# Long convolutions: four real products in PSUM, transform additions on VectorE, and full tables for the first inverse class

## The chip, the cores and the metric

The kernel runs on one core of one Trainium2 chip, as one launch. The metric is the device time in microseconds (us). Three runs of the kernel before gave 2213.26, 2218.42 and 2222.65 us; the median, 2218.42 us, is the time before.

## The reference

Two transformer layers run one after the other on a sequence of 1024 positions with 1024 channels, all in 32-bit floats. The first mixes dilated window attention with a Hyena branch, the second a state-space branch with latent attention. The change lies in the Hyena branch of the first layer alone: two rounds of a bidirectional long convolution over 512 channels, each followed by a gate, whose filters come from a small network.

```python
def bidirectional_long_conv(z, h_fwd, h_bwd):
    circ = jnp.concatenate([h_fwd, jnp.zeros((1, C), jnp.float32), h_bwd[:0:-1]], axis=0)
    hf = jnp.fft.rfft(circ, axis=0)
    zf = jnp.fft.rfft(z.astype(jnp.float32), n=2 * L, axis=1)
    y = jnp.fft.irfft(zf * hf[None], n=2 * L, axis=1)[:, :L]
...
    z = v
    for o, gate_o in enumerate((x1, x2)):
        z = gate_o * (bidirectional_long_conv(z, filters[:, o, 0], filters[:, o, 1]) + filt_bias[o] * z)
```

## The kernel before

**The transform.** Each convolution is done in the frequency domain, for 256 of the 512 channels at a time (`HC`), so there are four convolutions (two orders, two halves) and four transforms of filters. The 2048 frequencies are split by their residue modulo 16. Additions of 128x256 tiles (class `Fly`, lines 483 to 510, used by `fwd16`, `fwd8` and `inv8`) first make nine classes of inputs, of which classes 0 and 8 share one tile. A matrix product on TensorE with a table of cosines and sines then does the rest of each class: 128 positions in, 128 frequencies out, real and imaginary part side by side in a tile of 128 x 2 x 256. `inv8` puts the classes together again after the inverse products.

**Precision.** A matrix product of 32-bit floats is done with operands split into a high part (rounded to `fp32r`) and a low part (the rest): `split` casts on ScalarE (L176) and subtracts on VectorE or GpSimd (L181). `mm3` (L184 to L191) then issues three products, high by high, high by low, low by high, for each term.

**A transform of classes 1 to 7** (`transformed`, L654) multiplies a complex input by a complex table with three real products instead of four. `parts` (L616) first adds real and imaginary part on GpSimd (`sum`, L623), splits the sum on ScalarE and GpSimd, and splits the two parts themselves on ScalarE and VectorE. TensorE then forms one product of the sum (tile `ha`) and two others (tile `hx`), nine instructions of 256 columns in all. ScalarE copies `ha` out of PSUM (`sa`, L674), and VectorE adds it to both halves of `hx` (L675), which also brings the result to SBUF.

**The filters** (`filters`, L733): four rounds, each with 16 short products that give the filter's values, `fwd16`, and eight transforms, whose result `sp` is stored in DRAM.

**A convolution** (`long_conv`, L805) goes through the eight classes in the order 0, 4, 7, 1, 6, 2, 5, 3. `forward` splits the class, reads the filter's spectrum `hs` and transforms. `inverse` multiplies by the spectrum (L821 on VectorE; L822 on GpSimd, or on VectorE for class 0), combines on GpSimd (`zz`, L826 and L827), splits, and transforms back into a tile `wb`. When classes j and 8 - j are both back, their sum `sm` is formed on VectorE (L859) and their difference `df` on GpSimd (L860). Before the last two classes are transformed back, `fwd8` of the next convolution is written.

**The additions** of `Fly.tt` (L494) are given to VectorE and GpSimd in turn; the multiply-adds (L506) are all on VectorE.

**The first inverse class** holds classes 0 and 8 in one tile, 64 rows each. Twelve products (L843) work on half the rows each, in pairs for the two halves, and ScalarE copies the two results out (L845).

**What sets the order.** Each engine works through its own queue in a fixed order. The order is not written by hand: a scheduler places the instructions by the dependencies and its own estimates, and fills TensorE's gaps with projection products (`pj`, 512 columns) of later parts of the program, whose weights are read (`raw`), split (`wh`, `wl`) and whose results are evacuated by ScalarE (L983) and VectorE (`tr`, L984). Tiles have a fixed number of buffers, `HX` = 5 of them in PSUM for the transforms.

Of the kernel before, what the change touches and what calls it, by code (L numbers as in the profile page):

```python
# [9 lines left out]
F32 = mybir.dt.float32  # L10
# [6 lines left out]
P = 128  # L17
# [14 lines left out]
HC = 256  # L32
# [7 lines left out]
def constants():  # L40
# [18 lines left out]
    iv = np.zeros((8, 128, 3, 128))  # L59
# [24 lines left out]
    iv[0, 64:, 1] = -s8[:, :64].T / 1024  # L84
    rel = np.abs(np.arange(256)[None, :] - 64 - np.arange(128)[:, None])
# [396 lines left out]
class Fly:  # L482


    def __init__(self, k, bufs):
        self.nc, self.pool, self.n, self.bufs = k.nc, k.ypool, 0, bufs
# [4 lines left out]
    def tt(self, a, b, op, out=None):  # L491
        out = self.new() if out is None else out
        self.n += 1
        (self.nc.gpsimd if self.n % 2 == 0 else self.nc.vector).tensor_tensor(out, a, b, op=op)  # L494
        return out
# [77 lines left out]
def inv8(fl, w0, w8, w4, sm, df):  # L573

    A = {j: sm[j][:, 0] for j in (1, 2, 3)}
    Bp = {j: sm[j][:, 1] for j in (1, 2, 3)}
    Ap = {j: df[j][:, 0] for j in (1, 2, 3)}
    B = {j: df[j][:, 1] for j in (1, 2, 3)}
    c, c1, c3 = CS[2], CS[1], CS[3]
    s1, s3 = c3, c1  # L580
    x = [None] * 8
    a0, b0 = fl.add(w0, w8), fl.sub(w0, w8)
    p, n = fl.add(a0, w4[:, 0]), fl.sub(a0, w4[:, 0])
    g, h = fl.add(p, A[2]), fl.sub(p, A[2])
# [12 lines left out]
    x[3], x[5] = fl.add(u, v), fl.sub(u, v)  # L597
    return x
# [17 lines left out]
def parts(k, src, both=False):  # L616

    nc = k.nc
    n = 3 if both else 2
    hi, lo = (k.spl.tile([P, 3 if k.any else 2, HC], F32R, name="y" + x, tag="y" + x, bufs=k.bufs["y"]) for x in "hl")  # L620
    if both:
        t = k.spl.tile([P, HC], F32, name="sum", tag="sum", bufs=k.bufs["sum"])
        (nc.gpsimd if SUMP else nc.vector).tensor_add(t, src[:, 0], src[:, 1])  # L623
    split(nc, hi[:, :2], lo[:, :2], src)
    if both:
        split(nc, hi[:, 2], lo[:, 2], t, lo_eng="pool" if SUML else "dve")
    return [[t[:, c] for c in range(n)] for t in (hi, lo)]
# [21 lines left out]
FB = dict(y=2, sum=2, sa=1, t=2)  # L649
CB = dict(y=3, sum=2, sa=2, t=3)  # L650
LEADF = 1
DFP = 1
MULP = 1
# [5 lines left out]
def transformed(k, t, y, back, out):  # L659

    (th, tl), (yh, yl) = t, y
    nc = k.nc
    term = lambda b, c: (th[:, b, :], tl[:, b, :], yh[c], yl[c])
    ps = k.hps.tile([P, 2, HC], F32, name="hx", tag="hx", bufs=HX)
    if len(yh) < 3:
        mm3(nc, ps[:, 0], [term(0, 0), term(1, 1)])
        mm3(nc, ps[:, 1], [term(0, 1), term(2, 0)])
        return ps
    pa = k.hps.tile([P, 2, HC], F32, name="ha", tag="hx", bufs=HX)[:, 0]
    mm3(nc, pa, [term(0, 2)])  # L670
    mm3(nc, ps[:, 0], [term(1, 1)])
    mm3(nc, ps[:, 1], [term(2, 0)])
    sa = k.spl.tile([P, HC], F32, name="sa", tag="sa", bufs=k.bufs["sa"])
    nc.scalar.copy(sa, pa)  # L674
    nc.vector.tensor_add(out, ps, sa.unsqueeze(1).to_broadcast([P, 2, HC]))  # L675
    return out


def spectrum(k, y, j, out):

    if j:
        return transformed(k, table(k, "k_fw", j), y, 0, out)
    yh, yl = y
    ps = k.hps.tile([P, 2, HC], F32, name="hx", tag="hx", bufs=HX)
    ts = [table(k, "k_fw", c) for c in (0, 8)]
    for b in range(2):
        mm3(k.nc, ps[:, b], [(th[:, b, :], tl[:, b, :], yh[c], yl[c]) for c, (th, tl) in enumerate(ts)])
    return ps
# [41 lines left out]
def filters(k):  # L730
# [4 lines left out]
    with ExitStack() as es:  # L735
# [5 lines left out]
        k.bufs, k.any = FB, bool(KF)  # L741
# [27 lines left out]
        for n, (hf, o) in enumerate(rounds):  # L769
# [4 lines left out]
            ahead = [parts(k, y[j], j in KF) for j in ORDER[:LEADS]]  # L774
            for i, j in enumerate(ORDER):
                if i + LEADS < 8:
                    ahead.append(parts(k, y[ORDER[i + LEADS]], ORDER[i + LEADS] in KF))
# [28 lines left out]
def long_conv(k, y, o, hf, z):  # L806
# [5 lines left out]
    def forward(j):  # L812
        yp = parts(k, y[j], j in KZ)
        hs = k.hpl.tile([P, 2, HC], F32, name="hs", tag="hs")
        nc.sync.dma_start(hs, k.spec[o, hf, j])
        t2 = k.prd.tile([P, 2, HC], F32, name="t2", tag="t2", bufs=T2)
        return hs, t2, spectrum(k, yp, j, t2)

    def inverse(j, hs, t2, ps):
        zz = k.prd.tile([P, 2, HC], F32, name="zz", tag="zz", bufs=ZZ)  # L820
        nc.vector.tensor_mul(zz, ps, hs[:, 0:1].to_broadcast([P, 2, HC]))  # L821
        (nc.gpsimd if MULP and ps is t2 else nc.vector).tensor_mul(t2, ps, hs[:, 1:2].to_broadcast([P, 2, HC]))  # L822
# [27 lines left out]
    for i, j in enumerate(order):  # L850
# [5 lines left out]
        if 0 < j < 4:  # L856
# [3 lines left out]
            (nc.gpsimd if DFP and j in KI else nc.vector).tensor_sub(df[j], w[j], w[8 - j])  # L860
# [5 lines left out]
def hyena(k):  # L866
# [6 lines left out]
    with ExitStack() as es:  # L873
# [48 lines left out]
        k.ybufs, k.bufs, k.any = YB, CB, bool(KZ or KI)  # L922
# [1298 lines left out]
```

## Time and profile before

| What | us |
|---|---|
| median of 3 runs | 2218.42 |
| the profiled execution's own time | 2230.01 |
| its span, first to last instruction | 2228.2 |
| TensorE (PE) busy in the span | 2046.7 (92%) |
| VectorE (DVE) busy | 1489.1 (67%) |
| ScalarE (ACT) busy | 849.7 (38%) |
| GpSimd (POOL) busy | 782.4 (35%) |

All numbers of a trace come from the one profiled execution. Busy times are those in which an engine worked on at least one instruction. A product's own duration is longer than the distance to the next one, since products follow each other in a pipeline; how long a run of them takes is read from their starts. A wait is the idle time of an engine before an instruction, put down to whatever released it last. The granted clock is given as a share of full speed, 2.4 GHz; half of it is 1.2 GHz.

### The profile page before, as it was taken

The page shows a single profiled execution, that of the slowest core. Times are in us where ns is not written, and L with a number is a line of the kernel's source. Part 1 is how long each engine was busy: PE and PEld are TensorE (multiplying, and loading weights), DVE is VectorE, ACT ScalarE, POOL GpSimd, SP SyncE. Part 2 cuts the span into 40 slices and gives each one's busy share as a digit, 9 for nine tenths or more (in the row PEclk, how much of TensorE's full clock was granted, in tenths as well). Part 3 has the DMA queues.
Part 4 walks back from the last instruction along what each step waited for, and adds up shares of the span by engine and source line. Part 5 has one row for each costly group of instructions (what it writes and reads, how often), then busy time and mean ns, then how long its engine had stood idle before and what let it go on. Part 6 is the DMA issues. An engine that isn't in the chain of part 4 may idle for free. (4 is left out here: it accounts for less than half of the span.)

```text
span 2228.2 us, 30387 instructions
## 1 busy us (share of the span) xinstructions
PE 2046.7 (92%) x10421; PEld 1644.6 (74%) x10421; DVE 1489.1 (67%) x2814; ACT 849.7 (38%) x1802; POOL 782.4 (35%) x719
## 2 busy tenths in 40 slices
PE   4999989989798999989899998999899999999997
PEld 2777777778686787766677677778677777778787
DVE  8888888877989744242433326785786558875686
ACT  3523332333242325343444342334422335554433
POOL 3256555597787710001010101131255323401222
PEclk9999999999999999999999999999899999999999
DMA  7135655756564665454545237544445353436351
GB/s 292 62 108 201 187 179 183 238 184 204 157 198 142 210 188 137 109 114 114 118 100 121 59 92 229 200 146 138 134 140 167 96 169 95 127 113 197 121 170 53
DMA packets 222876, 333.74 MB, mean 150 GB/s; under 512 B 65690, under 2 KB 128704, under 8 KB 222722
## 3 DMA queue, kind: packets, MB, share of 16 engines
q1 hardware_dynamic: 212784, 325.18, 48.7%
q0 software_dynamic: 1952, 4.07, 0.8%
q10 hardware_dynamic: 7986, 2.56, 0.5%
q8 instruction: 82, 1.34, 0.3%
q14 instruction: 72, 0.59, 0.1%
HBM read 250.76 MB, written 79.78 MB: 148 GB/s over the span
## 5 line engine op out<-in xcount | busy, mean ns | idle before, releaser
L191 PE MATMUL pj<-hh,wh 128*128 128x512 f32 x1104 | 447.9, 406 | 17.9 <-DVE tr L984 15.2
L191 PE MATMUL pj<-hh,wl 128*128 128x512 f32 x1104 | 446.7, 405 | 0.1
L191 PE MATMUL pj<-hl,wh 128*128 128x512 f32 x1104 | 446.3, 404 | 0.0
L176 ACT CAST wh<-raw 128x1024 fp32r<-128x1024 f32 (+3 forms) x196 | 174.8, 896 | 331.5 <-PE pj L191 277.7
L181 DVE TENSOR_TENSOR wl<-raw,wh 128x1024 fp32r<-128x1024 f32 (+2 forms) x177 | 212.4, 1202 | 88.2 <-ACT wh L176 87.5
L191 PEld LDWEIGHTS pj<-hh,wh 128*128 128x128 f32 x1104 | 212.6, 193 | 67.4 <-DVE tr L984 12.8
L191 PEld LDWEIGHTS pj<-hh,wl 128*128 128x128 f32 x1104 | 212.5, 192 | 46.2 <-issue 0.7
L191 PEld LDWEIGHTS pj<-hl,wh 128*128 128x128 f32 x1104 | 213.1, 193 | 45.3 <-issue 0.5
L1139 DVE CUSTOM_DVE_ANT_0 sb<-s,tb 128x192 f32<-128x192 f32 (+2 forms) x192 | 63.2, 347 | 108.5 <-PE s L1138 102.5
L1142 ACT ACTIVATE sb<-sb,stat 128x192 f32<-128x192 f32 (+2 forms) x192 | 85.5, 447 | 88.2 <-DVE stat L1139 78.1
L1241 POOL TENSOR_TENSOR w<-w,og 128x1024 f32<-128x1024 f32 x3 | 7.2, 2386 | 314.0 <-ACT vn L1030 105.7
L1158 PE MATMUL po<-pT,vn 128*64 128x128 f32 (+1 forms) x640 | 113.1, 302 | 1.4 <-DVE pT L1028 1.4
L494 POOL TENSOR_TENSOR bt<-bt 128x256 f32<-128x256 f32 x88 | 87.7, 1019 | 60.3 <-DVE bt L494 42.4
L191 PE MATMUL pj<-xh,wl 128*128 128x512 f32 x256 | 103.8, 406 | 1.9 <-DVE wl L181 1.9
L181 POOL TENSOR_TENSOR yl<-sum,yh 128x256 fp32r<-128x256 f32 x84 | 85.9, 1029 | 52.3 <-ACT yh L176 52.3
L191 PE MATMUL pj<-xh,wh 128*128 128x512 f32 x256 | 103.5, 407 | 0.0
L191 PE MATMUL pj<-xl,wh 128*128 128x512 f32 x256 | 103.0, 402 | 0.0
L1028 DVE COPY pT<-pt 128x256 f32<-128x256 f32 (+4 forms) x72 | 32.1, 449 | 105.1 <-PE pt L1150 77.2
L1158 PEld LDWEIGHTS po<-pT,vn 128*64 128x64 f32 (+1 forms) x640 | 67.1, 142 | 47.2 <-issue 37.2
L1137 PE MATMUL s<-kh,qa 128*128 128x192 f32 (+2 forms) x192 | 58.0, 314 | 20.9 <-DVE stat L1139 20.0
L191 PE MATMUL hx<-yh,k_fw 128*128 128x256 f32 x288 | 67.8, 298 | 8.3 <-ACT yh L176 8.3
L1326 POOL TENSOR_TENSOR tg<-tg,tg 128x512 f32<-128x512 f32 x16 | 28.3, 1769 | 117.3 <-DVE rs_ve L201 58.3
(614 smaller groups left out, 5033.6 us busy)
## 6 DMA issues: line engine op xcount, KB each, us to landing
raw<-in_w_in_dram SPq DMA_DIRECT2D x92, 512.0 KB, 3.8
k_fw<-k_fw SPq DMA_DIRECT2D x56, 384.0 KB, 4.3
qkv<-tr SPq DMA_DIRECT2D x80, 256.0 KB, 3.3
raw<-in_w_out_dram SPq DMA_DIRECT2D x32, 512.0 KB, 3.6
k_iv<-k_iv SPq DMA_DIRECT2D x28, 384.0 KB, 3.9
row<-in_w_ada_dram SPq DMA_DIRECT2D x16, 512.0 KB, 5.8
dc<-in_k_decay_dram SPq DMA_DIRECT2D x64, 128.0 KB, 3.4
spec<-sp SPq DMA_DIRECT2D x32, 256.0 KB, 4.4
```

The costliest lines, as they stand in the source:

```text
L176: nc.scalar.copy(hi, src)
L181: (nc.vector if lo_eng == "dve" else nc.gpsimd).tensor_sub(lo, src, f(hi))
L191: nc.tensor.matmul(ps, a, b, start=(i == 0), stop=(i == n - 1))
L494: (self.nc.gpsimd if self.n % 2 == 0 else self.nc.vector).tensor_tensor(out, a, b, op=op)
L1028: nc.vector.tensor_copy(out, in_)
L1137: nc.tensor.matmul(ps[:, m, :n], qa[h][:, qt], kh[h][:, ks], start=True, stop=False)
L1139: nc.vector.tensor_tensor_reduce(sb[:, m, :n], ps[:, m, :n], tabs[h][:, off : off + n], -0.125, 3.0e38, op0=ALU.add, op1=ALU.min, accum_ou ...
L1142: nc.scalar.activation(sb[:, m, :n], sb[:, m, :n], AF.Exp, scale=-1.0, bias=stat[:, t, h, 0:1], accum_out=stat[:, t, h, 1:2])
L1158: nc.tensor.matmul(po[hs, (tp + m) % 4, :], vn[:n, c, hs], pT[:n, s_, :], start=(x == 0), stop=(x == len(mine) - 1))
L1241: (nc.gpsimd if g == 1 else nc.vector).tensor_mul(w, w, og[g])
L1326: nc.gpsimd.tensor_add(t, t, first[c])
```

## The change

It has three parts. (1) The complex products of classes 1 to 7 are made of four real products that TensorE adds up in PSUM: cosine by both parts at once, 512 columns wide, then sine by each part, 256 columns. There is no sum, no third split, no copy `sa` and no addition behind the products. Spectra of filters are copied by ScalarE; in the convolutions the two multiplications by `hs` read PSUM, both on VectorE, and so do the sum and the difference of classes 1 to 3, the difference now on VectorE; inverse classes 0 and 4 to 7 are copied by ScalarE. (2) All additions of `Fly.tt` are on VectorE. (3) The first inverse class uses two tables of 128 rows, of which the second has its lower half negated, so that the products give the sum and the difference `a0`, `b0` of the two classes, and `inv8` doesn't form them.

```diff
-    iv = np.zeros((8, 128, 3, 128))
+    iv = np.zeros((9, 128, 3, 128))
...
-        fw[j, :, 0], fw[j, :, 1], fw[j, :, 2] = c, s - c, -c - s
-        iv[j, :, 0], iv[j, :, 1], iv[j, :, 2] = c.T / 1024, (-c - s).T / 1024, (s - c).T / 1024
+        fw[j, :, 0], fw[j, :, 1], fw[j, :, 2] = c, s, -s
+        iv[j, :, 0], iv[j, :, 1], iv[j, :, 2] = c.T / 1024, -s.T / 1024, s.T / 1024
...
+    iv[8, :64], iv[8, 64:] = iv[0, :64], -iv[0, 64:]
...
-        (self.nc.gpsimd if self.n % 2 == 0 else self.nc.vector).tensor_tensor(out, a, b, op=op)
+        self.nc.vector.tensor_tensor(out, a, b, op=op)
...
-def inv8(fl, w0, w8, w4, sm, df):
+def inv8(fl, a0, b0, w4, sm, df):
...
-    a0, b0 = fl.add(w0, w8), fl.sub(w0, w8)
...
-def parts(k, src, both=False):
...
+def parts(k, src):
+
+    hi, lo = (k.spl.tile([P, 2, HC], F32R, name="y" + x, tag="y" + x, bufs=k.bufs["y"]) for x in "hl")
+    split(k.nc, hi, lo, src)
+    return hi, lo
...
+def transformed(k, t, y):
+
     ps = k.hps.tile([P, 2, HC], F32, name="hx", tag="hx", bufs=HX)
...
+    seq = [(a, b) for a, b in ((t[0], y[0]), (t[0], y[1]), (t[1], y[0]))]
+    for i, (a, b) in enumerate(seq):
+        k.nc.tensor.matmul(ps.rearrange("p c q -> p (c q)"), a[:, 0, :], b.rearrange("p c q -> p (c q)"), start=(i == 0),
+                           stop=False)
+    for c in range(2):
+        for i, (a, b) in enumerate(seq):
+            k.nc.tensor.matmul(ps[:, c], a[:, 1 + c, :], b[:, 1 - c], start=False, stop=(c == 1 and i == 2))
+    return ps
+
+
+def two_tables(k, name, y, sums):
+
+    ps = k.hps.tile([P, 2, HC], F32, name="hx", tag="hx", bufs=HX)
+    ts = [table(k, name, c) for c in (0, 8)]
+    for b in range(2):
+        mm3(k.nc, ps[:, b], [(th[:, v, :], tl[:, v, :], y[0][:, u], y[1][:, u]) for th, tl, u, v in sums(ts, b)])
+    return ps
...
-                ps = spectrum(k, ahead.pop(0), j, sp)
-                if ps is not sp:
-                    nc.scalar.copy(sp, ps)
+                nc.scalar.copy(sp, spectrum(k, ahead.pop(0), j))
...
         nc.vector.tensor_mul(zz, ps, hs[:, 0:1].to_broadcast([P, 2, HC]))
-        (nc.gpsimd if MULP and ps is t2 else nc.vector).tensor_mul(t2, ps, hs[:, 1:2].to_broadcast([P, 2, HC]))
+        nc.vector.tensor_mul(t2, ps, hs[:, 1:2].to_broadcast([P, 2, HC]))
...
+        zp = parts(k, zz)
         if j:
-            ps = transformed(k, table(k, "k_iv", j), zp, 1, w)
-            if 0 < j < 4 or ps is w:
+            ps = transformed(k, table(k, "k_iv", j), zp)
+            if j < 4:
                 return ps
...
+        else:
+            ps = two_tables(k, "k_iv", zp, lambda ts, b: [(*ts[b], c, c) for c in range(2)])
+        w = k.ypool.tile([P, 2, HC], F32, name="wb", tag="wb", bufs=WB)
+        nc.scalar.copy(w, ps)
         return w
...
-            (nc.gpsimd if DFP and j in KI else nc.vector).tensor_sub(df[j], w[j], w[8 - j])
+            nc.vector.tensor_sub(df[j], w[j], w[8 - j])
```

Two places show how the queues change. The first is VectorE's queue in the second convolution, where `fwd8` makes the next convolution's classes (`bt`, `y`) while the last inverse classes come back (`wb`). Before:

```order
L821 TENSOR_TENSOR zz<-t_4662,hs 128x512
L181 TENSOR_TENSOR wl<-raw,wh 128x1024
L494 TENSOR_TENSOR bt<-bt 128x256
L494 TENSOR_TENSOR bt<-wb 128x256
L494 TENSOR_TENSOR y_4580<-bt 128x256
L494 TENSOR_TENSOR y_4581<-bt 128x256
L506 SCALAR_TENSOR_TENSOR y_4585<-bt 128x256 x2
L506 SCALAR_TENSOR_TENSOR y_4584<-bt 128x256 x2
L675 TENSOR_TENSOR wb<-hx,sa 128x512
L494 TENSOR_TENSOR bt<-bt,wb 128x256
L984 SCALAR_TENSOR_TENSOR tr<-pj,cols,tr 128x512
```

And of the change, the same place (L182 is the low part, L955 the evacuation `tr`):

```order
L182 TENSOR_TENSOR wl<-raw,wh 128x1024
L955 SCALAR_TENSOR_TENSOR tr<-pj,cols,tr 128x512
L494 TENSOR_TENSOR bt<-bt 128x256 x3
L494 TENSOR_TENSOR bt<-wb 128x256 x2
L494 TENSOR_TENSOR y_4186<-bt 128x256 x2
L494 TENSOR_TENSOR y_4187<-bt 128x256 x2
L506 SCALAR_TENSOR_TENSOR y_4191<-bt 128x256
L506 SCALAR_TENSOR_TENSOR y_4190<-bt 128x256
...
L494 TENSOR_TENSOR bt<-bt,sm 128x256 x2
L955 SCALAR_TENSOR_TENSOR tr<-pj,cols,tr 128x512
```

The additions that stood singly, each with a partner on GpSimd, now stand in twos and threes on VectorE, and the addition behind the products (L675) is gone from between them.

The second place is TensorE's queue at an inverse transform (`k_iv`) and the next forward one (`k_fw`), in the first convolution. Before:

```order
L191 MATMUL pj<-hh_127,wl 128x512
L191 MATMUL ha<-yh,k_iv 128x256
L191 MATMUL hx<-yh,k_iv 128x256
L191 MATMUL hx<-yl,k_iv 128x256
L191 MATMUL ha<-yl,k_iv 128x256
...
L191 MATMUL hx<-yh,k_iv 128x256 x2
```

And of the change:

```order
L192 MATMUL pj<-hh_122,wl 128x512
...
L649 MATMUL hx<-yh,k_iv 128x512
L649 MATMUL hx<-yl,k_iv 128x512
...
L653 MATMUL hx<-yh,k_iv 128x256
L653 MATMUL hx<-yl,k_iv 128x256
L653 MATMUL hx<-yh,k_iv 128x256 x2
```

Nine products of 256 columns have become three of 512 and six of 256, all into one tile `hx`. Over the whole queue, 936 projection products of 512 columns stood between the first and the last inverse product, and 758 do now; the others stand behind the last one.

## Rows read from the trace of the kernel before

**Rows 1.** Windows: window, its length, busy us (instructions) of PE, PEld, DVE, ACT, POOL, then PEclk, DMA share, GB/s.
```profile
130.00:405.00 275.00, 250.57 (x1207) 206.70 (x1206) 237.56 (x358) 88.25 (x161) 163.59 (x152) 0.94 0.57 183
405.00:800.00 395.00, 358.49 (x1781) 293.96 (x1780) 330.57 (x463) 132.66 (x263) 299.51 (x294) 0.97 0.58 183
130.00:800.00 670.00, 609.06 (x2986) 500.66 (x2985) 568.13 (x820) 220.91 (x424) 463.10 (x445) 0.96 0.57 183
550.00:600.00 50.00, 38.83 (x194) 31.80 (x193) 48.01 (x64) 16.09 (x31) 41.01 (x41) 0.94 0.50 156
600.00:650.00 50.00, 49.77 (x253) 40.88 (x252) 42.30 (x62) 16.68 (x33) 36.18 (x35) 0.96 0.65 202
...
800.00:2228.00 1428.00, 1341.80 (x7013) 1071.62 (x7011) 812.29 (x1822) 574.36 (x1277) 284.13 (x238) 0.97 0.47 132
```

**Rows 2.** Waits of PE from 130 to 800 us: us in all, times, longest.
```profile
PE pj L191 <- DVE tr L984: 15.2, 3, 7.8
PE hx L191 <- DVE yl L181: 15.0, 8, 3.4
PE hx L191 <- ACT yh L176: 8.3, 4, 3.0
PE ha L191 <- POOL yl L181: 7.5, 10, 1.3
PE hx L760 <- DVE w4l L181: 3.8, 2, 2.7
PE ha L191 <- ACT yh L176: 2.8, 2, 1.7
PE ha L191 <- DMA k_fw<-k_fw: 2.2, 3, 1.7
```

**Rows 3.** Timeline of PE at full clock: start us, duration us, instruction.
```profile
606.43 0.28 PE L191 MATMUL hx<-yh,k_fw 128*128 128x256 f32 x1
606.55 0.39 PE L191 MATMUL pj<-hl,wh 128*128 128x512 f32 x1
...
607.48 0.39 PE L191 MATMUL pj<-hh,wl 128*128 128x512 f32 x1
```

**Rows 4.** Timeline of PE, end of a first inverse class, then the next transform.
```profile
436.26 0.40 PE L843 MATMUL ha<-yh,k_iv 64*128 64x256 f32 x4
...
436.82 0.39 PE L191 MATMUL ha<-yh,k_fw 128*128 128x256 f32 x1
```

**Rows 5.** Groups by form, 130 to 800 us, DVE and POOL: xcount | busy us, mean ns | idle.
```profile
L494 DVE TENSOR_TENSOR bt<-bt 128x256 f32<-128x256 f32 x88 | 64.2, 766 | 2.8 <-POOL bt L494 2.7
L181 DVE TENSOR_TENSOR yl<-y,yh 128x512 fp32r<-128x512 f32 x64 | 60.7, 957 | 0.3 <-ACT yh L176 0.3
L506 DVE SCALAR_TENSOR_TENSOR y<-bt 128x256 f32<-128x256 f32 x96 | 57.6, 657 | 0.0
L181 DVE TENSOR_TENSOR yl<-zz,yh 128x512 fp32r<-128x512 f32 x32 | 29.1, 909 | 25.4 <-ACT yh L176 25.4
L821 DVE TENSOR_TENSOR zz<-t,hs 128x512 f32<-128x512 f32 x28 | 26.4, 944 | 0.4
L675 DVE TENSOR_TENSOR wb<-hx,sa 128x512 f32<-128x512 f32 x28 | 19.1, 684 | 11.7 <-PE hx L191 7.4 <-ACT sa L674 4.3
...
L181 POOL TENSOR_TENSOR yl<-sum,yh 128x256 fp32r<-128x256 f32 x84 | 85.9, 1029 | 52.3 <-ACT yh L176 52.3
L827 POOL TENSOR_TENSOR zz<-zz,t 128x256 f32<-128x256 f32 x32 | 26.2, 819 | 0.0
```

**Rows 6.** Timeline of DVE and POOL near 608 us.
```profile
608.16 0.41 DVE L494 TENSOR_TENSOR bt<-df 128x256 f32<-128x256 f32 x1
608.32 1.73 POOL L494 TENSOR_TENSOR bt<-bt 128x256 f32<-128x256 f32 x2 [0.36 <-DVE bt L494]
608.50 0.95 DVE L494 TENSOR_TENSOR bt<-sm 128x256 f32<-128x256 f32 x1
```

**Rows 7.** Groups by form, ACT, 130 to 800 us.
```profile
L983 ACT ACTIVATE tr<-pj,cols 128x512 fp32r<-128x512 f32 x30 | 20.5, 685 | 29.8 <-PE pj L191 10.3 <-issue 10.2 <-PE hx L191 4.3
```

More of the change, by code (lines that the diff above doesn't have):

```diff
@@ L485, in __init__ @@
     def __init__(self, k, bufs):
-        self.nc, self.pool, self.n, self.bufs = k.nc, k.ypool, 0, bufs
+        self.nc, self.pool, self.bufs = k.nc, k.ypool, bufs
     def new(self):
@@ L613, in table @@
     return t[:, 0], t[:, 1]
-def parts(k, src, both=False):
[L618 to L627, printed above, removed]
+def parts(k, src):
+    hi, lo = (k.spl.tile([P, 2, HC], F32R, name="y" + x, tag="y" + x, bufs=k.bufs["y"]) for x in "hl")
+    split(k.nc, hi, lo, src)
+    return hi, lo
 RAW = "tab"
@@ L648 @@
 TB = 2
-FB = dict(y=2, sum=2, sa=1, t=2)
-CB = dict(y=3, sum=2, sa=2, t=3)
+FB = dict(y=2, t=2)
+CB = dict(y=3, t=3)
 LEADF = 1
-DFP = 1
-MULP = 1
 WLOF = "dve"
@@ L656, with spectrum @@
 WLOA = "dve"
[L659 to L663, printed above, removed]
+def transformed(k, t, y):
     ps = k.hps.tile([P, 2, HC], F32, name="hx", tag="hx", bufs=HX)
[L665 to L679, printed above, removed]
-    if j:
[L682 to L688, printed above, removed]
+    seq = [(a, b) for a, b in ((t[0], y[0]), (t[0], y[1]), (t[1], y[0]))]
[12 more added lines that the diff above has]
+    return ps
+def spectrum(k, y, j):
+    if j:
+        return transformed(k, table(k, "k_fw", j), y)
+    return two_tables(k, "k_fw", y, lambda ts, b: [(*t, c, b) for c, t in enumerate(ts)])
 def new_y(k, order):
@@ L740, in filters @@
         k.spl = es.enter_context(tile_pool(tc, name="fspl", bufs=2))
-        k.bufs, k.any = FB, bool(KF)
+        k.bufs = FB
         fl = Fly(k, FLYF)
@@ L773, in filters @@
             xs = []
-            ahead = [parts(k, y[j], j in KF) for j in ORDER[:LEADS]]
+            ahead = [parts(k, y[j]) for j in ORDER[:LEADS]]
             for i, j in enumerate(ORDER):
                 if i + LEADS < 8:
-                    ahead.append(parts(k, y[ORDER[i + LEADS]], ORDER[i + LEADS] in KF))
+                    ahead.append(parts(k, y[ORDER[i + LEADS]]))
                 sp = k.spl.tile([P, 2, HC], F32, name="sp", tag="sp", bufs=2)
-                ps = spectrum(k, ahead.pop(0), j, sp)
-                if ps is not sp:
-                    nc.scalar.copy(sp, ps)
+                nc.scalar.copy(sp, spectrum(k, ahead.pop(0), j))
                 (nc.gpsimd if SPQ else nc.sync).dma_start(k.spec[o, hf, j], sp)
@@ L812, in forward, with inverse @@
     def forward(j):
-        yp = parts(k, y[j], j in KZ)
+        yp = parts(k, y[j])
         hs = k.hpl.tile([P, 2, HC], F32, name="hs", tag="hs")
         nc.sync.dma_start(hs, k.spec[o, hf, j])
+        return hs, spectrum(k, yp, j)
+    def inverse(j, hs, ps):
+        zz = k.prd.tile([P, 2, HC], F32, name="zz", tag="zz", bufs=ZZ)
         t2 = k.prd.tile([P, 2, HC], F32, name="t2", tag="t2", bufs=T2)
-        return hs, t2, spectrum(k, yp, j, t2)
-    def inverse(j, hs, t2, ps):
-        zz = k.prd.tile([P, 2, HC], F32, name="zz", tag="zz", bufs=ZZ)
         nc.vector.tensor_mul(zz, ps, hs[:, 0:1].to_broadcast([P, 2, HC]))
-        (nc.gpsimd if MULP and ps is t2 else nc.vector).tensor_mul(t2, ps, hs[:, 1:2].to_broadcast([P, 2, HC]))
+        nc.vector.tensor_mul(t2, ps, hs[:, 1:2].to_broadcast([P, 2, HC]))
         if j == 0:
@@ L921, in hyena @@
         k.ypool = pool("yp", 1)
[L922 removed]
+        k.ybufs, k.bufs = YB, CB
         k.tab, k.spl, k.hpl, k.prd = pool("tab", 2), pool("spl", 2), pool("hpl", HB), pool("prd", 2)
```

20 lines of the change are left out of this document (removed).

## The prediction

> **What bounds the kernel now.** First the windows [rows 1]. The transforms of the filters (130 to 405 us) and the four long convolutions (405 to 800) take 670 us, and in them TensorE is busy 609.1 us, VectorE 568.1 and GpSimd 463.1. TensorE is the fullest, so the next question is what its idle 61 us wait for. The waits of that stretch [rows 2] answer: 15.2 us in only three waits for an evacuation on VectorE (L984), 15.0 and 3.8 for VectorE's low parts (L181), 11.1 for ScalarE's high parts, 7.5 for the low part of the sum on GpSimd. So VectorE ends some 34 of the 61, though on average it is not full. The reader should see in the narrow windows why: from 550 to 600 VectorE is busy 48.0 of 50 us and TensorE only 38.8; from 600 to 650, at 42.3, TensorE is busy 49.8. VectorE fills up in places, and TensorE waits there. Beside the waits stands the clock: 0.94 granted in the filters, 0.97 in the convolutions, where half clock (1.2 of 2.4 GHz) followed the idle stretches; that is 0.06 x 275 + 0.03 x 395 = 28 us lost. Together 89 us can be won back in this stage. A measurement of this kernel tells about 0.5%, 11 us, from no change.
>
> **TensorE, added.** There are 84 transforms of classes 1 to 7 (28 of filters, 28 forward, 28 inverse; the sum's low part counts them, x84 [rows 5]). Each had nine products of 256 columns and now has six of 256 and three of 512, the same number of instructions. At full clock a product of 256 is followed by the next after 0.12 us, and four of 512 take 607.48 - 606.55 = 0.93 us, 0.233 each [rows 3], so each transform grows by 3 x (0.233 - 0.12) = 0.34 us, and 84 by 28.5. The first inverse class ran its 12 products in pairs on half the rows each: eight of them take 436.82 - 436.26 = 0.56 us, 0.07 each [rows 4]; on all rows they take 0.12 each, 12 x 0.05 = 0.6 us, four times 2.4. TensorE gets **+31 us**. None of it has cover where TensorE is full.
>
> **VectorE, removed.** The 84 additions behind the products (L675, 0.68 us [rows 5]) go: -57 us. More goes with GpSimd's work. A 128x256 addition took 0.41 us when GpSimd stood still and 0.95 us when a GpSimd addition ran beside it [rows 6]. The means say the same: 0.766 for L494, 0.657 for L506's y, 0.957 and 0.909 for low parts that need 0.68 (the length of L675, which reads PSUM and does not stretch), 0.944 for zz [rows 5]. Over these five rows the excess is 88 x 0.36 + 96 x 0.25 + 64 x 0.28 + 32 x 0.23 + 28 x 0.26 = 88 us, 0.19 us for each busy us of GpSimd. After the change GpSimd keeps the two combinations per class (64 of 0.82 us, 52 us) and a few table splits. These 52 us cost VectorE 10; bounds are 0, if the queues never meet, and 52, if each holds VectorE for its whole length. I take 10, by the mean rate, since nothing makes these two meet oftener than others did. Relief: 78.
>
> **VectorE, added.** 144 of the transform's additions stood on GpSimd; eight (the a0 and b0 of four convolutions, four on each engine) disappear, so VectorE gets 136 more, 136 x 0.41 = 56. It gets the second multiplication by the spectrum, 28 x 0.68 = 19 (priced by the row that reads PSUM, L675, as it does now), and 12 differences, 12 x 0.68 = 8. Sum for VectorE: -57 - 78 + 83 = **-52 us**, from 568 to some 516.
>
> By the Trainium skill (SBUF — State Buffer, section "SBUF: two separate sides") VectorE and GpSimd share a port pair under an exclusive lock, held for a whole instruction by whoever starts first, so that the other blocks fully; by that rule alone the sum of the paragraph before the last would carry the upper bound, 52, and VectorE would fall by 10 us only. The trace agrees that the two collide but shows less than full blocking: 0.95 instead of 0.41, 0.54 us longer beside a GpSimd addition of 0.87 [rows 6].
>
> **GpSimd and ScalarE.** GpSimd loses the sums, their low parts, half the additions, the multiplications: what TensorE and ScalarE waited for there gets early, and nothing new is put in front of the 64 combinations. ScalarE loses 84 casts and 84 copies and gets 28 spectrum copies and 20 whole copies of inverse classes in place of 8 halves; at 0.685 us for 128x512 out of PSUM [rows 7] the 48 are 33 us, on an engine busy 221 of 670 [rows 1]: zero. The extra table of the first inverse class is one more load, split and store, then three reads; they are asked for ahead in SyncE's queue and TensorE waited 2.2 us in all for stored tables [rows 2], so between 0 and 2 us; I take 0. Its bound from below is 0 also, as nothing is removed.
>
> **What moves.** The order shows that between the first and the last inverse product stand 758 projection products of 512 columns instead of 936. These 178, 41 us at 0.233, run behind the convolutions. TensorE does them at the same pace there (1341.8 busy of 1428 [rows 1]). So the convolutions must shrink by more than 41 us, else the cover is missing and TensorE waits for VectorE where it worked before.
>
> **Sum.** Of the 61 us of waits: GpSimd's 7.5 go wholly. Of VectorE's 34, bounds 0 and 34, I take three fifths, 20: over the same 670 us VectorE's mean share falls from 85% to 77%, below the 85% of the stretch in which TensorE lost 0.2 us, but its one queue now holds both halves of each run of additions in front of the evacuations and low parts. Of ScalarE's 11, half, 5.5: what it waited for was often GpSimd. That is 33; the clock gives back in proportion, 28 x 33/61 = 15. Net 31 - 48 = **-17 us**. The profiled execution took 2230.0 us, so 2213; the median of the runs lies 11.6 us below it, so **2201 us**. By stages: filters 275 to about 266, convolutions 395 to about 345, and 41 more behind them. What is late next is TensorE itself, and the chain zz, combination, high part, low part of each inverse class.
>
> **Rivals.** *No change.* Only a third of the 89 us comes back, 31: 2218. For it: ScalarE's and VectorE's waits are chains, and a chain of one class stays four engines long. Against it: the three long waits for L984 come from a full VectorE.
> *All of it comes back.* Both loaded engines are relieved and the real order of the queues fits: 31 - 89 = -58, 2160. Against it: outside this stage, with VectorE busy 812 of 1428 us, TensorE still idles 6% [rows 1].
> *Slower, the cover is gone.* Projection products worth 41 us leave the convolutions, and the convolutions shorten by only half of VectorE's relief, 26 us, because both halves of the additions of one transform now stand in one queue ahead of zz; the filters keep their 10 us of added products less 5 that GpSimd's sums gave: 41 - 26 + 5 = +20, 2238. It decides in the stretches where the next convolution's classes are formed while the last inverse classes run (550 to 600 and its like), and from the point at which the convolutions take more than some 355 us. For it: VectorE's queue before and after is the only feeder of zz. Against it: the same stretch loses its stretched additions.
> *Slower, the two engines block each other in full.* Each remaining combination holds VectorE for 0.82 us, VectorE falls by 10 only, TensorE gets back GpSimd's 7.5 and 3 of clock: 31 - 10 = +21, 2239. Against it the 0.95 us of the row above. The Trainium skill's lock (the same section) would give this time; the trace bears it out only in part.
> That the edits do not do what they say I leave out: order and diff show the counts.
>
> **Chances.** Forecast 0.40, all of it back 0.12, no change 0.24, cover gone 0.17, full blocking 0.07. So faster by over 0.5% 0.52, within 0.5% 0.24, slower 0.24. The forecast's own range is 2180 to 2207. The 8 in 10 range takes in the case below down to 2165, and the cases above to 2240; half of the two slower cases and some of the fastest are left out.
>
> **What would show it.** Right: L494 and L506 on VectorE at 0.41 to 0.45 us, low parts at 0.7, VectorE's busy time in the two stages lower although its instructions are more, GpSimd nearly empty in the convolutions, no long wait for L984, products of 512 and 256 at 0.233 and 0.12, last inverse before about 750 us. Wrong: TensorE's waits for VectorE in the convolutions as large as now, half clock as often, or VectorE's additions still at 0.7 us and more.

## The result and the profile after

The changed kernel takes 2167.3 us (median of 4 runs, 2159.9 to 2172.8) where the kernel before, on the same chip, takes 2220.5 (4 runs). The ratio is 0.976 (95%: 0.974 to 0.978): **faster by 53 us, 2.4%**. The forecast was -17 us. The time lies outside the forecast's own range (2180 to 2207), by some 2 us inside the 8 in 10 range (2165 to 2240), and near the rival in which everything comes back (2160).

The page of the profiled execution after (2159.9 us, the lowest of its runs): span, busy times, and the rows of VectorE and GpSimd in 40 slices of the span.

```profile
span 2157.8 us, 29766 instructions
...
PE 2040.6 (95%) x10421; PEld 1645.9 (76%) x10421; DVE 1368.3 (63%) x2906; ACT 819.7 (38%) x1675; POOL 419.2 (19%) x368
...
DVE  8987767788786232343424338694876558885686
POOL 3201210231221000010100102050454333401222
```

VectorE was busy 1489.1 us and is busy 1368.3; GpSimd went from 782.4 to 419.2. TensorE's busy time hardly moved (2046.7 and 2040.6), although its products cost more: the granted clock of the whole span rose from 0.964 to 0.979.

From here on "the stage" is the time from 130 us to the last inverse product. It ended at 780 us before and ends at 678 now. The windows of the kernel before, cut at its own marks, stage and remainder (columns as in [rows 1]), and in front of them its part up to the first inverse product, which is the mark between filters and convolutions from here on:

```profile
130.00:435.00 305.00, 279.28 (x1338) 229.28 (x1336) 263.81 (x407) 96.51 (x175) 183.87 (x172) 0.95 0.57 184
...
130.00:780.00 650.00, 589.06 (x2899) 484.62 (x2898) 552.03 (x793) 216.00 (x417) 455.41 (x437) 0.96 0.58 184
...
780.00:2228.00 1448.00, 1361.80 (x7101) 1087.66 (x7099) 828.39 (x1849) 579.27 (x1284) 291.82 (x246) 0.97 0.47 133
```

And of the changed kernel: filters, convolutions, the stage as a whole, the remainder.

```profile
130.00:408.00 278.00, 273.83 (x1328) 227.87 (x1327) 212.12 (x464) 93.04 (x146) 38.43 (x27) 0.99 0.61 203
408.00:678.00 270.00, 269.90 (x1384) 227.06 (x1383) 212.35 (x406) 84.63 (x134) 65.70 (x67) 1.00 0.68 222
130.00:678.00 548.00, 543.74 (x2710) 454.93 (x2709) 424.48 (x870) 177.67 (x280) 104.13 (x94) 0.99 0.65 212
678.00:2157.00 1479.00, 1399.48 (x7288) 1117.33 (x7286) 835.13 (x1865) 587.35 (x1294) 279.92 (x238) 0.97 0.47 133
```

The reader is to see three things. TensorE's idle time in the stage (length less busy) fell from 60.9 to 4.3 us, and its clock rose from 0.96 to 0.99. VectorE carries out 77 instructions more in 128 us less. By parts, the filters went from 305 to 278 us and the convolutions from 345 to 270. And behind the stage there are 31 us more, with 187 more TensorE instructions: the projection products that moved. In sum the stage is 102 us shorter and the span 70; the medians differ by 53, since the profiled execution is the changed kernel's fastest, and the one before was slower than all four of its runs.

[Rows 2] has seven waits of 2 us and more. Of the changed kernel, 130 to 690 us, the same view has one line:

```profile
PE hx L742 <- DVE bt L744: 4.2, 1, 4.2
```

The groups of VectorE by form in the stage, against [rows 5] (xcount | busy us, mean ns | idle before):

```profile
L494 DVE TENSOR_TENSOR bt<-bt 128x256 f32<-128x256 f32 x168 | 60.1, 418 | 0.2
L182 DVE TENSOR_TENSOR wl<-raw,wh 128x1024 fp32r<-128x1024 f32 x35 | 46.4, 1327 | 7.2 <-ACT wh L177 7.1
L182 DVE TENSOR_TENSOR yl<-y,yh 128x512 fp32r<-128x512 f32 x64 | 45.5, 719 | 17.0 <-ACT yh L177 16.9
L506 DVE SCALAR_TENSOR_TENSOR y<-bt 128x256 f32<-128x256 f32 x96 | 35.2, 429 | 0.0
L506 DVE SCALAR_TENSOR_TENSOR bt<-bt 128x256 f32<-128x256 f32 x70 | 25.4, 419 | 0.0
L182 DVE TENSOR_TENSOR yl<-zz,yh 128x512 fp32r<-128x512 f32 x32 | 22.1, 691 | 17.6 <-ACT yh L177 17.5
L801 DVE TENSOR_TENSOR zz<-hx,hs 128x512 f32<-128x512 f32 x32 | 21.9, 685 | 7.7 <-PE hx L653 4.9 <-PE hx L192 2.5
```

The five rows that the prediction took for the relief now stand near their undisturbed length: additions L494 0.418 us instead of 0.766, `y` 0.429 instead of 0.657, low parts 0.719 and 0.691 instead of 0.957 and 0.909, `zz` 0.685 instead of 0.944.

TensorE's price is as forecast. Its timeline inside a transform (L649: cosine, 512 columns; L653: sine, 256): a start follows the other after 0.23 us, then after 0.12.

```profile
553.23 0.40 PE L649 MATMUL hx<-yl,k_fw 128*128 128x512 f32 x1
553.46 0.40 PE L649 MATMUL hx<-yh,k_fw 128*128 128x512 f32 x1
553.69 0.28 PE L653 MATMUL hx<-yh,k_fw 128*128 128x256 f32 x1
553.81 0.27 PE L653 MATMUL hx<-yl,k_fw 128*128 128x256 f32 x1
```

### The profile page after: what moved, and what is told of

It is laid out like the page before. It is cut to its first block, busy times and chain, and to the rows that moved or that the text cites. A ratio compares the mean times of both kernels' runs of the same rounds, so it can differ in the third digit from the quotient of the medians.

```text
span 2157.8 us, 29766 instructions
## 1 busy us (share of the span) xinstructions
PE 2040.6 (95%) x10421; PEld 1645.9 (76%) x10421; DVE 1368.3 (63%) x2906; ACT 819.7 (38%) x1675; POOL 419.2 (19%) x368
## 5 line engine op out<-in xcount | busy, mean ns | idle before, releaser
L192 PE MATMUL pj<-hh,wh 128*128 128x512 f32 x1104 | 440.9, 399 | 2.9 <-DVE kl L1046 2.9
L192 PE MATMUL pj<-hh,wl 128*128 128x512 f32 x1104 | 440.8, 399 | 0.1
L192 PE MATMUL pj<-hl,wh 128*128 128x512 f32 x1104 | 440.5, 399 | 0.0
L182 DVE TENSOR_TENSOR wl<-raw,wh 128x1024 fp32r<-128x1024 f32 (+2 forms) x177 | 206.5, 1169 | 116.2 <-ACT wh L177 115.7
L806 POOL TENSOR_TENSOR zz<-zz,t 128x256 f32<-128x256 f32 x32 | 33.9, 1060 | 182.1 <-DVE t L802 141.6
L494 DVE TENSOR_TENSOR bt<-bt 128x256 f32<-128x256 f32 x176 | 63.3, 418 | 0.4
L1121 PE MATMUL pt<-idn,sb 128*128 128x128 f32 (+1 forms) x320 | 61.8, 297 | 1.1 <-ACT vn L1001 0.7
L192 PEld LDWEIGHTS pj<-xh,wl 128*128 128x128 f32 x256 | 48.7, 190 | 13.1 <-DVE wl L182 1.0
```

What stands on the lines that cost most here:

```text
L182: (nc.vector if lo_eng == "dve" else nc.gpsimd).tensor_sub(lo, src, f(hi))
L192: nc.tensor.matmul(ps, a, b, start=(i == 0), stop=(i == n - 1))
L494: self.nc.vector.tensor_tensor(out, a, b, op=op)
L806: nc.gpsimd.tensor_sub(zz[:, 0], zz[:, 0], t2[:, 1])
L1121: nc.tensor.transpose(pst[:n, s_, :], sb[:, m, a : a + n], k.idn)
```

## The experiments

The open question was why nearly all waits went. Three theories stood at the start. **A**: VectorE's load, its stretching by GpSimd's work counted in. **B**: the long chain of a transform by three products (sum, third split, copy `sa`, addition L675), gone with part 1. **C**: the additions of one run handed to and fro between VectorE and GpSimd, gone with part 2. A fourth, **D**, was formed after the first runs: what counts is that GpSimd's work beside VectorE makes single VectorE instructions longer, not how full VectorE is.

### The parts one by one

**e1_additions**: the kernel before, with part 2 alone (`Fly.tt`).

```diff
-        (self.nc.gpsimd if self.n % 2 == 0 else self.nc.vector).tensor_tensor(out, a, b, op=op)
+        self.nc.vector.tensor_tensor(out, a, b, op=op)
```

> The kernel before with one edit: all additions of the transforms on VectorE (part 2 alone). Theory A (VectorE was late because of its load, to which GpSimd's neighbouring work adds by stretching VectorE's instructions): 144 additions at 0.41 us are +59 us on VectorE, and some 141 us less of GpSimd work beside it take back about 40, so VectorE is as full as before: 2210 to 2235 us. Theory B (the long chain of a transform by three products, sum, cast, low part, copy, addition, held TensorE up, whoever does the steps): no gain either, 2210 to 2230. Theory C (what held TensorE up was the handing to and fro of additions between two engines): most of the gain, 2175 to 2195.

Measured: 2227.2 us, ratio 1.0023 (1.001 to 1.0037): no gain, if anything 5 us lost. **e2_products**: part 1 alone; additions alternate as before, the first inverse class has its half tables. The diff is that of the change without `tt` and `k_iv`'s ninth table.

> Part 1 of the change alone: four real products in PSUM, but additions given to VectorE and GpSimd in turn, and the first inverse class by half tables. Theory A: GpSimd loses some 300 us of its 463 in the two stages and VectorE its 84 additions behind the products, so nearly all of the gain: 2165 to 2185 us. Theory B: the chain is short, 2165 to 2180. Theory C: the alternation is still there, 2205 to 2225.

Measured: 2201.4 us, ratio 0.991 (0.988 to 0.993): some 20 of the 53 us. **e3_three_on_vector**: still three products per transform, with all that GpSimd did for them moved to VectorE, but for the 64 combinations and the table splits.

```diff
-        (self.nc.gpsimd if self.n % 2 == 0 else self.nc.vector).tensor_tensor(out, a, b, op=op)
+        self.nc.vector.tensor_tensor(out, a, b, op=op)
...
-SUMP = 1
-SUML = 1
+SUMP = 0
+SUML = 0
...
-DFP = 1
-MULP = 1
+DFP = 0
+MULP = 0
```

> Three products as before, but GpSimd's share of the transforms (sum, low part of the sum, second multiplication, difference, half the additions) all on VectorE, so that nothing but the 64 combinations and the table splits stands beside it. Theory A: no stretching any more, but 463 us of GpSimd work become some 190 us on VectorE: VectorE is as full as before (540 us and more busy in the two stages), 2205 to 2240 us. Theory B: the chain's steps on VectorE take 0.41 instead of 1.03 to 1.08 us each, the chain gets shorter and the time falls, 2180 to 2200.

Measured: 2201.9 us, ratio 0.990 (0.988 to 0.993). Stage and remainder of e1, then e2's stage, then e3's stage and remainder:

```profile
130.00:780.00 650.00, 612.23 (x3047) 504.66 (x3047) 529.78 (x938) 223.04 (x428) 355.29 (x300) 0.98 0.60 192
780.00:2220.00 1440.00, 1324.90 (x6951) 1056.71 (x6949) 826.06 (x1849) 571.52 (x1273) 282.09 (x239) 0.96 0.47 130
```
```profile
130.00:688.00 558.00, 529.35 (x2598) 434.66 (x2597) 439.03 (x736) 171.57 (x276) 240.38 (x230) 0.98 0.62 200
```
```profile
130.00:763.00 633.00, 616.04 (x3112) 514.05 (x3110) 550.91 (x1146) 226.14 (x430) 107.02 (x93) 0.98 0.62 199
763.00:2200.00 1437.00, 1312.36 (x6886) 1046.07 (x6885) 819.62 (x1848) 569.29 (x1271) 281.73 (x238) 0.95 0.46 129
```

e2 and e3 make a pair. In e2 VectorE is busy 439 of 558 us (79%), much as in the changed kernel (424 of 548, 77%), yet TensorE idles 28.7 us and not 4.3; GpSimd is busy 240. In e3 VectorE is busy 551 us, as much as before the change and 87% of the stage, yet TensorE idles 17.0 and not 60.9; GpSimd is down to 107. So TensorE's idle time does not follow VectorE's load, and A as a matter of load missed both, e3 by 3 us only. C missed e1: without any handing to and fro 37.8 us of idle time stay. B missed e2, which has the short chain and still loses 29, and e3 by 2 us, so e3's total alone decides little; its stage says more.

What does go along with it is how long GpSimd works in the stage: 455 us before, 355 in e1, 240 in e2, 107 in e3 and 104 after the change, with 60.9, 37.8, 28.7, 17.0 and 4.3 us of TensorE's idle time. The length of VectorE's instructions goes along as well, though not that of one form alone. `y` (L506, x96; 0.657 us before, 0.429 after) in e2 and in e3:

```profile
L506 DVE SCALAR_TENSOR_TENSOR y<-bt 128x256 f32<-128x256 f32 x96 | 44.3, 517 | 0.0
```
```profile
L506 DVE SCALAR_TENSOR_TENSOR y<-bt 128x256 f32<-128x256 f32 x96 | 34.2, 413 | 0.0
```

In e1 `y` takes 0.469 us, less than in e2, and yet TensorE idles more; but the low parts `yl` stand at 0.880 and 0.791 us in e1 and at 0.752 and 0.738 in e2. e3 has `y` at its free length and GpSimd as little busy as the changed kernel, yet idles 17.0 us against 4.3. These 13 us can hardly be GpSimd's doing; TensorE's largest waits there are for tables (5.6 us), ScalarE's high parts (5.4) and VectorE's low parts (3.1), and whether the longer chain or the fuller VectorE makes them was not separated.

Why do e1 and e3 win more of TensorE's idle time in the stage than they gain in all? The order put more of other work into their stage (3047 and 3112 TensorE instructions in all, 2899 before), and behind it TensorE, with less to do, idles 115 and 125 us, against 86 before. TensorE's waits in e3 from 763 to 900 us:

```profile
PE t L945 <- DVE bt L494: 12.3, 3, 6.3
PE s L1137 <- DMA kh<-qkv: 10.0, 1, 10.0
PE t L945 <- DVE xg L946: 9.4, 3, 4.3
```

`t` (L945) transposes the results of the last convolution on their way out; from 780 to 900 us the kernel before has no wait longer than 0.6 us. So what e3 won in the stage it partly gave back right behind it. That the projection products that were used up earlier are missing there as cover for the end of the last convolution fits the counts; it was not tested by itself. In e1 two of the three waits stand there as well (780 to 900 us): 10.8 us for `xg` and 9.9 for `kh`.

**e4_class0**: the changed kernel with part 3 undone (half tables, `a0` and `b0` formed again).

```diff
-            ps = two_tables(k, "k_iv", zp, lambda ts, b: [(*ts[b], c, c) for c in range(2)])
...
+                for i in range(2):
+                    r = slice(64 * i, 64 * i + 64)
+                    nc.tensor.matmul(ps[i], u[r, c], v[r, c], start=(x == 0), stop=(x == 5))
```

> The changed kernel with part 3 undone: the first inverse class by half tables in pairs, a0 and b0 formed by eight additions on VectorE. With TensorE full in the convolutions its 2.4 us less of products count and VectorE's 8 x 0.41 = 3.3 us more don't: 2163 to 2168 us, against 2167 of the changed kernel, that is no difference. If the first inverse class held the convolutions up by itself, the time moves by more than 10 us.

Measured: 2171.2 us, ratio 0.977 (0.975 to 0.979), the changed kernel's own within the interval. Part 3 weighs nothing that can be told.

### Giving GpSimd work that nobody reads

**e6_idle_pool**: the changed kernel, and GpSimd adds beside it, 96 times 128x512 and 140 times 128x256, into tiles that nothing reads. (The additions do read live tiles, `y`, `zz`, `bt`.)

```diff
+        self.n += 1
+        if self.n % 2 == 0:
+            t = self.pool.tile([P, HC], F32, name="dead", tag="dead", bufs=2)
+            self.nc.gpsimd.tensor_tensor(t, out, out, op=op)
...
+    t = k.spl.tile([P, 2, HC], F32, name="idle", tag="idle", bufs=2)
+    k.nc.gpsimd.tensor_add(t, src, src)
```

> The changed kernel with work on GpSimd whose results nobody reads: an addition of 128x512 behind each split of a transform's input (96), and one of 128x256 behind every second addition of the transforms (140). GpSimd is then about as busy in the two stages as in the kernel before, but no other engine waits for its results. Theory A (GpSimd's neighbouring work stretches VectorE, and that made VectorE late): VectorE's additions take 0.6 us and more in the mean, its busy time in the two stages rises by 70 to 110 us, TensorE's waits come back in part: 2180 to 2205 us. Theory B (the chain of three products): the chain is as short as in the changed kernel, so 2165 to 2175.

Measured: 2241.9 us, ratio 1.007 (1.005 to 1.010): by the ratios, (1.007 - 0.976) x 2220, some 70 us slower than the changed kernel, and slower than the kernel before. **e9_half_idle** has only the 96 larger additions.

> The changed kernel with only the 96 unread additions of 128x512 on GpSimd, without those behind the transforms' additions: half the dose of the run with 236 of them. Theory D: stretching about 60 to 75 us over the two stages instead of 25 and 123, and TensorE's time lost there about 40 us instead of 13 and 87: 2185 to 2210 us. Theory A: VectorE's busy time rises by some 40 us to 465 of 570, still with room: 2165 to 2180.

Measured: 2205.7 us, ratio 0.989 (0.988 to 0.991), inside what D expected (2185 to 2210) and outside A's 2165 to 2180. Filters, then convolutions, of e9 and of e6:

```profile
130.00:431.00 301.00, 284.75 (x1346) 232.37 (x1345) 238.21 (x466) 93.31 (x146) 113.69 (x65) 0.98 0.58 188
431.00:715.00 284.00, 276.11 (x1399) 229.22 (x1398) 240.51 (x407) 85.37 (x135) 144.36 (x126) 1.00 0.66 213
```
```profile
130.00:459.00 329.00, 292.69 (x1346) 237.41 (x1345) 267.49 (x463) 91.75 (x146) 182.59 (x147) 0.96 0.52 170
459.00:761.00 302.00, 281.90 (x1397) 232.98 (x1396) 258.01 (x409) 86.58 (x138) 185.96 (x177) 0.98 0.63 203
```

The filters are the cleaner half: of the arithmetic of the transforms nothing stands on GpSimd there, so none of it queues behind the added work. Only tables do (`k_fw`): waits for their splits and loads are 7.4 of e9's 16.2 us of idle time and 5.3 of e6's 36.3. VectorE's number of instructions hardly moves (464, 466, 463). GpSimd's busy time goes 38, 114, 183 us; VectorE's 212, 238, 267; TensorE's idle time 4.2, 16.2, 36.3; the filters' length 278, 301, 329. In e6 VectorE's additions L494 there take 0.586 us, and TensorE waits for what VectorE and ScalarE split:

```profile
L494 DVE TENSOR_TENSOR bt<-bt 128x256 f32<-128x256 f32 x133 | 69.6, 586 | 0.0
```
```profile
PE hx L192 <- DVE yl L182: 10.0, 4, 4.1
PE hx L192 <- ACT yh L177: 6.9, 2, 4.0
PE hx L655 <- DVE yl L182: 4.5, 2, 4.2
PE hx L655 <- DVE wl L182: 4.3, 1, 4.3
```

The kernel before, cut at the same mark (130 to 435 us, above), has nearly e6's busy times there, GpSimd 184 and VectorE 264 us, and 25.7 us of idle time, with the same two waits at the head: 11.1 us for VectorE's `yl` and 8.3 for ScalarE's `yh`, and only 0.3 for GpSimd's own low part. Two other ways in which the added work could act are small in the filters: VectorE waited once, 1.1 us, until GpSimd had read a tile that was to be written anew, and ScalarE's instructions keep their length (`yh` 0.623 us in e6, 0.622 in the changed kernel). So GpSimd's concurrent work alone, whose results nobody reads, brings back waits of the kind of [rows 2]. A had the right sign for e6 but expected too little (2180 to 2205); B, by which next to nothing should have moved (2165 to 2175), fell. In the convolutions the 64 combinations stand behind the added work in GpSimd's queue, so there the two causes are not apart.

**e10_hybrid**: the changed kernel, whose 28 transforms of filters go by three products again, everything for them on VectorE and ScalarE, with tables `k_f3` of their own.

```diff
-            ahead = [parts(k, y[j]) for j in ORDER[:LEADS]]
+            ahead = [parts3(k, y[j], j) for j in ORDER[:LEADS]]
...
-                nc.scalar.copy(sp, spectrum(k, ahead.pop(0), j))
+                spectrum3(k, ahead.pop(0), j, sp)
```

> The changed kernel, but the 28 transforms of filters by three products again, with sum, low part and final addition all on VectorE, and seven tables more. Theory D (what held TensorE up was GpSimd's work stretching VectorE's instructions, not VectorE's load): VectorE gets 28 x 1.5 = 42 us more in the filters, where it has room, without stretching, and TensorE's products get 28 x 0.34 = 9.5 us shorter: 2155 to 2164 us, 3 to 12 below the changed kernel. Theory A (VectorE's load): the filters' waits come back by 10 us and more, 2168 to 2185. Theory B (the chain of three products): the filters' waits come back as in the kernel before, 2185 and more.

**e12_changed_again** is the changed kernel once more, beside e9 and e10.

> The changed kernel once more, for comparison on the same chip: ratio to the kernel before 0.974 to 0.979.

Measured: e10 2167.2 us, ratio 0.973 (0.972 to 0.974); e12 2169.6, ratio 0.975 (0.972 to 0.977). The two cannot be told apart, so e10 is no better kernel. B expected 2185 or more of e10, and fell. D's 2155 to 2164 was missed too: the gain of TensorE's cheaper filters did not show. Its filters and convolutions:

```profile
130.00:435.00 305.00, 302.04 (x1495) 251.44 (x1494) 259.94 (x558) 106.07 (x187) 40.10 (x29) 1.00 0.63 202
435.00:722.00 287.00, 280.01 (x1410) 234.22 (x1410) 211.30 (x404) 87.43 (x140) 73.62 (x72) 0.99 0.67 216
```

VectorE is busy 48 us longer in the filters than in the changed kernel and TensorE idles there no more than in that kernel (3.0 us and 4.2), with VectorE 85% busy: load alone did no harm there. The convolutions idle 7.0 us where the changed kernel idled 0.1. Why is not settled.

e12's stage, in its own profile, is as long as the first; the remainder is 17 us longer (1496 to 1479), which is all the difference between the two profiled executions:

```profile
130.00:678.00 548.00, 542.90 (x2709) 453.68 (x2708) 423.08 (x870) 177.47 (x280) 105.81 (x94) 1.00 0.65 212
678.00:2174.00 1496.00, 1408.43 (x7288) 1125.22 (x7286) 835.93 (x1865) 587.57 (x1294) 283.56 (x238) 0.97 0.46 131
```

**e7_narrow**: the changed kernel, with each product of 512 columns cut into two of 256.

```diff
...
+            k.nc.tensor.matmul(ps[:, c], a[:, 0, :], b[:, c], start=(i == 0), stop=False)
...
```

> The changed kernel with its 84 x 3 products of 512 columns cut into 84 x 6 of 256. TensorE is busy without a gap in the convolutions, so only its own time counts: 84 x 3 x (2 x 0.12 - 0.233) = +1.8 us, 2167 to 2172 us. If the gain came from the wide products (fewer instructions, fewer weight loads per column), 2180 us and more.

Measured: 2179.2 us, ratio 0.978 (0.976 to 0.980). By the ratio it is the changed kernel's time or some 5 us more. (The 2179.2 themselves lie just under the 2180 named for the wide products, but the kernel before was 7 us slower beside this run as well.) The width of the products is not where the gain lies.

### The collision by itself

**e8_collision** leaves the whole computation out and runs rows of subtractions of 128x256 on VectorE and GpSimd: VectorE alone, both, VectorE reading one operand from PSUM, and copies.

> VectorE and GpSimd alone, everything else left out: 40 subtractions of 128x256 on VectorE with GpSimd idle, then 80 with both inputs in SBUF, 80 with one input in PSUM and 80 copies, while GpSimd does 221 subtractions of 128x256 of its own. Partial stretching, as in the kernel before: VectorE's subtractions 0.41 us alone and 0.7 to 1.0 beside GpSimd, those that read PSUM and the copies 0.41 or less, unmoved. Full blocking, one instruction of either engine at a time: each of the 80 takes its own 0.41 plus GpSimd's 0.75, 1.15 us and more, and GpSimd's own get longer by as much as VectorE uses.

VectorE's lines: durations (least, median, greatest, ns), starts of the first and the last.

```profile
L2163 DVE TENSOR_TENSOR s<-s,s x120: 408/937/946, 3.8 to 93.9; 128x256 f32<-128x256 f32 x120
L2163 DVE TENSOR_TENSOR s<-ps,s x80: 408/408/424, 92.1 to 120.7; 128x256 f32<-128x256 f32 x80
L2165 DVE COPY s<-s x80: 275/278/47437, 121.0 to 193.6; 128x256 f32<-128x256 f32 x80
```

Alone 0.408 us; beside GpSimd 0.94, that of [rows 6]; with one operand in PSUM 0.408 beside GpSimd as well. That is partial stretching, not the 1.15 us of full blocking; but the copies, expected unmoved, had one that stood for 47 us. **e11_copies** repeats it with copies and multiply-adds (again nothing else of the kernel).

> VectorE and GpSimd alone again: 40 copies of 128x256 on VectorE with GpSimd idle, 20 copies against 61 subtractions on GpSimd, then 40 multiply-adds with two SBUF inputs against 61 more. In the earlier run one copy stood for 47 us beside a row of GpSimd subtractions. If a copy really gets no turn while GpSimd's instructions follow each other without a gap, the first copy of the second group lasts 35 us and more, until GpSimd's row ends. If that was an accident of that run, copies take 0.3 to 1.0 us each. Multiply-adds: 0.9 us each beside GpSimd, as the subtractions did.

Beside GpSimd a copy takes 0.81 us and a multiply-add 0.94. Alone they take 0.28 and 0.43. So the copies got their turn this time, within the 0.3 to 1.0 us expected for that case, and copies are not unmoved beside GpSimd. Subtraction, copy and multiply-add each have their price with and without GpSimd, apart from a stall that is told below.

## Why the prediction was right or wrong

**Right, TensorE, added (+31), as far as its spacings go.** Products of 512 follow each other after 0.23 us and of 256 after 0.12, as [rows 3] had it. e7 and e4 show that neither width nor part 3 carries more than a few us.

**Right, ScalarE and the extra table at zero.** No wait for either is left in the stage. **Right, what moves**: 178 products, 41 us; the remainder is 31 us longer in one profile and 48 in the other.

**Mis-sized, VectorE's relief (-52).** In the stage VectorE's busy time fell by 552.0 - 424.5 = 128 us. The price of the removed additions was right (x83 of L675 in the kernel before, 57 us), and so were the five rows taken for the relief: 22 + 15 + 7 + 7 us for `y`, the two low parts and `zz`, where 24, 18, 7 and 7 were taken, and 62.0 - 84 x 0.36 = 32 for the additions L494, where 32 was taken. (The reading of [rows 6] was loose in one point: GpSimd did not stand still during the addition of 0.41 us, it began 0.16 us after it.) What failed is "over these five rows": other forms of the same kind stretched too and were left out. In the stage of the kernel before they stood as

```profile
L181 DVE TENSOR_TENSOR wl<-raw,wh 128x1024 fp32r<-128x1024 f32 x39 | 57.6, 1476 | 6.6 <-ACT wh L176 6.5
L506 DVE SCALAR_TENSOR_TENSOR bt<-bt 128x256 f32<-128x256 f32 x70 | 31.9, 507 | 0.4
L506 DVE SCALAR_TENSOR_TENSOR bt<-bt,z 128x256 f32<-128x256 f32 x32 | 20.6, 694 | 0.1
L494 DVE TENSOR_TENSOR y<-bt 128x256 f32<-128x256 f32 x16 | 12.4, 812 | 0.0
```

and their means are now 1.327, 0.419, 0.433 and 0.417: 39 x 0.15 + 70 x 0.09 + 32 x 0.26 + 16 x 0.40 = 27 us, and a dozen smaller forms bring as much again. Some 9 us more (four `wl`, five `tr`) left the stage with the projections. What was added cost 76 and not 83, as an L494 adds 60.1 / 168 = 0.36 us of busy time and not its length. Together: -57 - 84 - 54 - 9 + 76 = -128. The 10 us charged for the combinations that stayed on GpSimd were of the right size: against the shortest means of the other runs `wl` is still 35 x 0.10 us too long, `yl` 64 x 0.03, `y` 96 x 0.02, and small forms add a few us; some 10 in all, an estimate.

**Wrong, the share of the waits that comes back.** "Of VectorE's 34 ... I take three fifths, 20", because its mean share falls to 77%. The share did fall to 77%, but it is not what decides: e3 has 87% and loses 17 us, e2 has 79% and loses 29, and e10's filters have 85% and lose 3. Nearly all came back: the idle time fell by 60.9 - 4.3 = 57 us and the clock gave 650 x 0.04 - 548 x 0.01 = 21, together 78 where 48 was taken. The forecast's own sum with that number is 31 - 78 = -47, against -53 measured. So the half of the mechanism that says that GpSimd's work stretches VectorE, TensorE waits and the clock falls was right. The step that failed is the one that turned VectorE's relief into TensorE's waits: the prediction had VectorE fill up in places, held on to two fifths of the waits because it would still be fairly full, and let the clock follow in proportion. The runs show 57 of 61 us gone: 44 of them go in e3 already, which moves GpSimd's share to a VectorE no emptier than before, the other 13 only with the rest of the change.

**The rivals.** "All of it comes back" (2160) was nearly the case; its argument against, TensorE's 6% of idle time outside the stage, spoke of another stage. "The cover is gone" did not come true here, as the stage shrank by 102 us and not by less than 41; but idle time can move in that way: e1 and e3 win 23 and 44 us of TensorE's idle time before the last inverse product and lose 29 and 38 behind it. "Full blocking" fell: VectorE's forms are near their free length although GpSimd is busy 104 us in the stage, and e8 has 0.94 us and not 1.15.

**Open.** Why longer VectorE instructions cost TensorE more than a fuller VectorE was not separated: it may be results that come late at single places, or an order fixed in advance with lengths that the collision breaks. The 13 us that e3 idles more than the changed kernel are open too. e10's convolutions are open as said.

## What to carry to other kernels

Work given to GpSimd is paid for on VectorE. Here a 128x256 instruction with two SBUF operands took 0.41 us alone and 0.94 beside GpSimd, and with GpSimd busy 70% of the stage the means of the larger groups of such forms lay between (0.51 to 0.81). Count that over every form and not the largest five, and look for forms that read one operand from PSUM, which kept their length here. An engine's mean busy share doesn't say what its waits are worth; an experiment that adds work nobody reads on the suspected engine (e9, e6) does. Where a change empties one stage, look at what fill it has left for the next.

## What the runs showed of the hardware that was not expected

**The collision is an alternation.** In e11, a copy and a multiply-add on VectorE beside GpSimd's row:

```profile
28.85 0.81 DVE L2165 COPY s<-s 128x256 f32<-128x256 f32 x1
29.58 0.94 DVE L2176 SCALAR_TENSOR_TENSOR s<-s,s 128x256 f32<-128x256 f32 x1
```

The copy, which reads a single operand, is held up as well. In e8 VectorE's and GpSimd's subtractions each start every 0.86 us (window, its length, busy us and instructions of VectorE, then of GpSimd):

```profile
30.00:90.00 60.00, 60.00 (x71) 60.00 (x70) 1.00 0.00 0
```

While VectorE stands idle or stalled, GpSimd's start every 0.68 us: GpSimd pays as well. The Trainium skill (SBUF — State Buffer, section "SBUF: two separate sides") has the two engines exclude each other for whole instructions; 0.86 us is less than 0.41 + 0.68, the sum that this would give, and less than 0.34 + 0.68, where 0.34 is VectorE's distance from start to start in e8 with GpSimd idle. So these rows show a turn for each, but not an exclusion over the whole length, and the measurement decides.

**A turn can be lost for long.** One copy of e8 took 47.4 us (the greatest value above), and in e11 a row of VectorE that began 0.07 us after GpSimd's stood still at its first multiply-add for 26.1 us:

```profile
64.41 35.37 POOL L2174 TENSOR_TENSOR g<-g,g 128x256 f32<-128x256 f32 x49
64.48 39.66 DVE L2176 SCALAR_TENSOR_TENSOR s<-s,s 128x256 f32<-128x256 f32 x20 [16.25 <-POOL g L2172]
```

In both cases GpSimd's row ran without a gap meanwhile. What decides between alternation and stall was not found. The kernel before has no such stall: its longest L494 took 1.52 us.

**Unread work can cost more than the whole change brings**: e6's 70 us against 53.
